# Two unused tiles that shift the right half of SBUF: 224 bytes for every pool there, 128 more for one

## The chip, the cores and the metric

The kernel runs on one core of a Trainium2 chip. The metric is the device time of one execution in microseconds (us). SBUF, the on-chip memory, has 128 partitions; an address below is the byte offset inside a partition, the same for all 128.

## The reference

One layer of a decoder trunk over 2,048 tokens of width 1,024, in float32, batch 1:

```python
mod = silu(c) @ w_ada + b_ada                      # shift, scale, gate, twice
u = rmsnorm(h, norm1_w) * (1 + sc1) + sh1
hq, hf, hi, hg, aq, ak, av = split(u @ w_in)       # 1024 -> 3584
o_hg = hgrn2(hq, hf, hi, hg)                       # 4 heads, state 128x128, chunks
o_da = diff_attention(aq, ak, av)                  # 4 heads, 2 softmaxes each, causal, ALiBi
h = h + g1 * (concat(o_hg, o_da) @ w_out)
u = rmsnorm(h, norm2_w) * (1 + sc2) + sh2
h = h + g2 * ((silu(u @ w_gate) * (u @ w_up)) @ w_down)   # inner width 2816
return rmsnorm(h, final_norm_w)
```

## The kernel before

**Products in three parts.** Nearly all matrix products are made with the type float32r. Every operand is split (`split`, L114 and L115) into a high part, a cast by ACT, and a low part, the rest, which DVE subtracts. A product is then three matmuls: high by high, high by low, low by high. Of a matmul, one operand is stationary (128 x 128, loaded into the array by a weight load that runs beside the matmul before it) and one is moving (128 x 256 or 128 x 512, streamed through).

**The lines with the matmuls.**

- L162, in `proj_ft`: 24 matmuls of 512 columns per accumulation; stationary are the weights wh and wl, moving the activations uh and ul. It serves attention's queries and keys and the recurrence's q and f. L408 is the same at the start of the kernel.
- L174, in `proj_tf`: 24 matmuls of 256 columns per accumulation, two accumulations a call; stationary are the activations, moving the weights. It serves the values, the recurrence's i and g, and the output projection.
- L603 and L604, attention's scores: stationary is q, moving ks, up to 512 columns.
- L629 and L633: attention's transposes and its product with the values, in plain float32, 128 columns.
- L985, in `seven`: the gate and up projections. A 2 x 2 block product is made with seven products in place of eight, each of 12 matmuls with 512 columns; stationary are the weights or their sums (wh2 and wl2; sh and sl for the seventh product), moving combinations of the activations (cx, cy, cu, ct2, ct3, ct4). In the first product the last matmul is cut into two halves of 256 columns. `seven` is called 44 times: two halves of the tokens, 11 pairs of weight blocks, gate and up.
- L1079, in `down`: the down projection, four blocks of 512 tokens, 22 inner blocks each, 24 matmuls of 512 columns for one; stationary are the activations sh and sl, moving the weights wh2 and wl2.

**The stages.** From 0 to some 400 us the norms and attention's projections; to some 1,130 us attention, with the recurrence and its projections put between its steps; then the output projection; and from some 1,400 us on the feed-forward part for the second half of the tokens (`seven`, then `down`), and again for the first half. TensorE's instructions run in the order of the program. The tile framework sets all waits, by the tiles that instructions read and write and by the memory that a tile takes over from an older one.

**Where tiles lie.** Pools are stacked from two sides. On the left, from address 16,512 on: the constants, puA, and then, one stage after the other, puB and px, pk and pp, pu7 and pt5. On the right, from 229,344 downwards: pw and pwD, ph, pf, px2, ps. Inside a pool the tiles lie in the order of their first use, from low addresses to high, each rounded up to 32 bytes. Nearly all large tiles have a multiple of 512 bytes, so one number says where the operands of a pool start:

| Pool | Side | What of it goes into matmuls | Start modulo 512 |
| --- | --- | --- | --- |
| puA, puB, pu7 | left | activations: uh, ul, all of cx, cy, cu, ct2, ct3, ct4 | 256 |
| pk | left | ks, q, the values vt | 256 |
| const | left | ident | 128 |
| pp | left | s, wt | 256, 96 |
| pw, pwD, pf | right | weights: wh, wl, wh2, wl2 | 480 |
| ph | right | the recurrence's Q, K, KM, KT | 352 |
| ps | right | sh, sl | 96 |

Between the lowest right pool and the highest left one there are at least 2,496 free bytes in every stage.

Of the kernel before, what the change touches and what calls it, by code (L numbers as in the profile page):

```python
# [9 lines left out]
F32 = mybir.dt.float32  # L10
# [9 lines left out]
P = 128  # L20
# [28 lines left out]
def kernel(ctx: ExitStack, tc: tile.TileContext, io: dict, out: bass.AP):  # L49
# [12 lines left out]
    dram = ctx.enter_context(tc.tile_pool(name="dram", bufs=1, space=DRAM))  # L62
    psum = ctx.enter_context(tc.tile_pool(name="psum", bufs=1, space=PSUM))
    puA = ctx.enter_context(tc.tile_pool(name="puA", bufs=1))
    early, later = ExitStack(), ExitStack()
    pw = early.enter_context(tc.tile_pool(name="pw", bufs=2, side="right"))

    def bank(tag, bufs, shape=(512,)):
        return psum.tile([P, *shape], F32, name=f"ps_{tag}", tag=tag, bufs=bufs)
# [16 lines left out]
    def bcast_row(ap):  # L86
        return ap.partition_broadcast(P)
# [745 lines left out]
    ps = ctx.enter_context(tc.tile_pool(name="ps", bufs=1, side="right"))  # L833

    def slots(names):

        n = [0]

        def take(dt=F32):
            two = []  # L840
            for c in range(2):
                tag = names[n[0] % len(names)]
                n[0] += 1
                two.append((puA if tag[0] == "u" else pu7).tile([P, TB], dt, name="slot", tag=tag, bufs=1))
            return two
        return take
# [104 lines left out]
    def temp():  # L951
        return pt5.tile([P, TB], F32, name="t512", tag="t512", bufs=NTMP)
# [89 lines left out]
    def down_step(b, f, at):  # L1042

        t = at()
        SP.dma_start(out=t, in_=act_d[b][f])
        return f, split_small(t), split_big(load_big(w_down[f * P:(f + 1) * P, None, :], 1))

    def down(b, at, first, others=(), after=()):

        others = iter(others)
        tags = (("acc", 2), ("acc", 2), ("sc", 2), ("sc", 2), ("hg", 2), ("hg", 2), ("pv", 1), ("tr", 1))
        pds = [bank(*t) for t in tags]
        place = slots([f"u{z}{k}" for z in "hl" for k in range(4)])
        ho = [place() for tt in range(NT)]
        place = slots(T4[4:])
        fw, g2 = place(), place()
        ws = []
        for f in range(NF):  # L1060
            ws.append(first.pop(0) if first else down_step(b, f, at))
            next(others, None)
            if f == 8:
                for c in range(2):
                    cs = slice(c * TB, (c + 1) * TB)
                    SP.dma_start(out=g2[c], in_=gate_d[1][:, cs])
                    SP.dma_start(out=fw[c], in_=bcast_row(io["final_norm_w"][cs]))
                    for tt in range(NT):
                        SP.dma_start(out=ho[tt][c], in_=h_d[b][tt * P:(tt + 1) * P, cs])

            if NF - (LAST if b else LAST0) <= f < NF - 1:
                continue
            for tt in range(NT):
                tsl = slice(tt * P, (tt + 1) * P)
                for cc in ((0,), (1,)) if not b and f == NF - 1 else ((0, 1),):
                    for g, a, w in ws:
                        for m, (x, y) in enumerate(((0, 0), (0, 1), (1, 0))):
                            for c in cc:
                                PE.matmul(  # L1079
                                    pds[2 * tt + c], a[x][:, tsl], w[y][:, c * TB:(c + 1) * TB],  # L1080
                                    start=g == 0 and m == 0, stop=g == NF - 1 and m == 2,
                                )
            ws = []
        for _ in others:
            pass
        made = after() if after else None

        def norm(tt):
            ss = ps.tile([P, 2], F32, name="fss", tag="fss", bufs=4)
            for c in range(2):  # L1090
                junk = ps.tile([P, TB], BF16, name="junk", tag="junk", bufs=1)
                ACT.activation(junk, ho[tt][c], AF.Square, accum_out=ss[:, c:c + 1])
            r = ps.tile([P, 1], F32, name="f_r", tag="f_r", bufs=2)
            DVE.tensor_tensor(r, ss[:, 0:1], ss[:, 1:2], op=ALU.add)
            DVE.tensor_scalar(r, r, 1.0 / D, EPS, op0=ALU.mult, op1=ALU.add)
            POOL.tensor_tensor(r, r, mhalf[:, :1], op=ALU.pow)
            for c in range(2):
                DVE.scalar_tensor_tensor(ho[tt][c], ho[tt][c], r, fw[c], op0=ALU.mult, op1=ALU.mult)
                (POOL if b else SP).dma_start(
                    out=out[0, b * TB + tt * P:b * TB + (tt + 1) * P, c * TB:(c + 1) * TB], in_=ho[tt][c]  # L1100
                )

        for tt in range(NT):
            ts = [temp() for c in range(2)]
            for c in range(2):
                DVE.tensor_tensor(ts[c], pds[2 * tt + c], g2[c], op=ALU.mult)
                if not b:
                    DVE.tensor_tensor(ho[tt][c], ho[tt][c], ts[c], op=ALU.add)
            if b:
                for c in range(2):  # L1110
                    DVE.tensor_tensor(ho[tt][c], ho[tt][c], ts[c], op=ALU.add)
            if not b:
                norm(tt)
        return made, (lambda: [norm(tt) for tt in range(NT)]) if b else None

    def calls(*fs):

        for f in fs:
            f()
            yield  # L1120
# [21 lines left out]
    two = [down_step(1, f, at1) for f in range(2)]  # L1142
    two, norms = down(1, at1, two, after=lambda: [down_step(0, f, at0) for f in range(2)])
    down(0, at0, two, calls(norms))


_INS = [
# [38 lines left out]
```

## Time and profile before

| What | Value |
| --- | --- |
| Time of 3 runs | 2808.2, 2809.4 and 2815.19 us, median 2809.4 |
| The profiled execution | 2806.66 us, of it the span 2804.8 us |
| Mean granted TensorE clock | 0.988 of full |
| TensorE busy | 2706.7 us, 97% of the span |
| Weight loads busy | 2320.0 us, 83% |
| DVE, ACT, POOL busy | 1709.4, 1124.3, 327.4 us |
| DMA | 403.52 MB, mean 144 GB/s |

PE is TensorE's matmuls, PEld its weight loads, DVE VectorE, ACT ScalarE, POOL GpSimd, SP SyncE, which issues most DMAs. The matmuls are pipelined: one starts before the one ahead has ended, so the duration of one is longer than its distance to the next. "L985" is line 985 of the kernel. `ps_acc<-cxh,wh` is a matmul that writes the PSUM tile ps_acc from moving cxh and stationary wh. The chain of waits is followed back from the last instruction, at each step to what released it.

### The profile page before, as it was taken

The page shows a single profiled execution, that of the slowest core. Times are in us where ns is not written, and L with a number is a line of the kernel's source. Part 1 is how long each engine was busy: PE and PEld are TensorE (multiplying, and loading weights), DVE is VectorE, ACT ScalarE, POOL GpSimd, SP SyncE. Part 2 cuts the span into 40 slices and gives each one's busy share as a digit, 9 for nine tenths or more (in the row PEclk, how much of TensorE's full clock was granted, in tenths as well). Part 3 has the DMA queues.
Part 4 walks back from the last instruction along what each step waited for, and adds up shares of the span by engine and source line. Part 5 has one row for each costly group of instructions (what it writes and reads, how often), then busy time and mean ns, then how long its engine had stood idle before and what let it go on. Part 6 is the DMA issues. An engine that isn't in the chain of part 4 may idle for free.

```text
span 2804.8 us, 40363 instructions
## 1 busy us (share of the span) xinstructions
PE 2706.7 (97%) x15017; PEld 2320.0 (83%) x15017; DVE 1709.4 (61%) x3456; ACT 1124.3 (40%) x2062; POOL 327.4 (12%) x493
## 2 busy tenths in 40 slices
PE   6999999999999998898999999999999999999998
PEld 5888879999999997897878888878887888888886
DVE  6434557777777779664585555553757555554354
ACT  4542135565565666543342222242433222222232
POOL 2552200000010000112210000020101000000010
PEclk9999999999999999998999999999999999999999
DMA  8765672434234220656542222274845222226461
GB/s 274 262 210 171 215 224 79 136 121 132 80 117 143 72 91 31 220 178 224 171 129 89 76 75 83 83 281 150 299 132 162 86 75 79 79 83 221 140 217 61
DMA packets 306104, 403.52 MB, mean 144 GB/s; under 512 B 22970, under 2 KB 208620, under 8 KB 305780
## 3 DMA queue, kind: packets, MB, share of 16 engines
q1 hardware_dynamic: 276788, 307.60, 34.4%
q0 software_dynamic: 29120, 93.35, 9.0%
q8 instruction: 118, 1.93, 0.3%
q14 instruction: 78, 0.64, 0.1%
HBM read 309.63 MB, written 91.23 MB: 143 GB/s over the span
## 4 chain that ended last, share of the span: by engine, by line
PE 74%; DMA 4%; DVE 4%; issue 3%; ACT 1%; POOL 1%; SPq 0%; POOLq 0%; DVEq 0%; ACTq 0%
PE ps_sc L985 8%; PE ps_hg L985 8%; PE ps_acc L985 8%; PE ps_acc L174 8%; PE ps_acc L162 5%; PE ps_acc L1079 4%; PE ps_sc L1079 4%; PE ps_hg L1079 4%; PE ps_pv L633 4%; PE ps_pv L1079 2%; PE ps_tr L985 2%; PE ps_pv L985 2%; PE ps_tr L1079 2%; PE ps_tr L629 2%; PE ps_sc L603 2%
## 5 line engine op out<-in xcount | busy, mean ns | idle before, releaser
L115 DVE TENSOR_TENSOR wl<-wraw,wh 128x1024 fp32r<-128x1024 f32 x252 | 307.5, 1221 | 98.4 <-ACT wh L114 94.9
L114 ACT CAST wh<-wraw 128x1024 fp32r<-128x1024 f32 x252 | 263.6, 1047 | 221.3 <-PE ps_acc L174 111.5
L174 PE MATMUL ps_acc<-wh,uh 128*128 128x256 f32 x1040 | 295.5, 286 | 0.8 <-ACT uh L505 0.6
L174 PE MATMUL ps_acc<-wl,uh 128*128 128x256 f32 x1040 | 293.8, 284 | 2.1 <-DVE wl L115 2.1
L174 PE MATMUL ps_acc<-wh,ul 128*128 128x256 f32 x1040 | 292.3, 284 | 0.0
L114 ACT CAST wh<-wsum 128x1024 fp32r<-128x1024 f32 x88 | 92.3, 1049 | 307.5 <-issue 142.7
L174 PEld LDWEIGHTS ps_acc<-wl,uh 128*128 128x128 f32 x1040 | 196.0, 189 | 4.9 <-DVE wl L115 2.3
L174 PEld LDWEIGHTS ps_acc<-wh,uh 128*128 128x128 f32 x1040 | 195.7, 189 | 3.8 <-ACT uh L505 1.4
L174 PEld LDWEIGHTS ps_acc<-wh,ul 128*128 128x128 f32 x1040 | 194.9, 189 | 2.3 <-issue 0.2
L115 DVE TENSOR_TENSOR sl<-slot,sh 128x512 fp32r<-128x512 f32 x88 | 60.5, 690 | 203.3 <-ACT sh L114 200.0
L612 ACT ACTIVATE s<-s,mx 128x2048 f32<-128x2048 f32 (+15 forms) x128 | 154.0, 1203 | 47.0 <-DVE mx L607 45.3
L607 DVE CUSTOM_DVE_ANT_0 s<-ps_sc,dist,mx 128x512 f32<-128x512 f32 x192 | 143.5, 748 | 44.1 <-PE ps_sc L604 39.6
L114 ACT CAST sh<-slot 128x512 fp32r<-128x512 f32 x88 | 54.2, 620 | 259.2 <-PE ps_tr L1079 217.5
L633 PE MATMUL ps_pv<-vt,wt 128*128 128x128 f32 x1088 | 150.8, 278 | 3.3 <-ACT wt L631 3.1
L633 PEld LDWEIGHTS ps_pv<-vt,wt 128*128 128x128 f32 x1088 | 140.4, 194 | 11.0 <-ACT wt L631 5.9
L115 DVE TENSOR_TENSOR wl<-wsum,wh 128x1024 fp32r<-128x1024 f32 x88 | 107.5, 1222 | 68.7 <-ACT wh L114 65.7
L162 PE MATMUL ps_acc<-ul,wh 128*128 128x512 f32 x352 | 141.9, 404 | 1.0 <-DMA ul<-ud 1.0
L162 PE MATMUL ps_acc<-uh,wh 128*128 128x512 f32 x352 | 142.1, 406 | 0.0
L1027 POOL DMA_DIRECT2D actd<-t x88 | 47.9, 544 | 798.1 <-DVE t L1026 793.8
L162 PE MATMUL ps_acc<-uh,wl 128*128 128x512 f32 x352 | 140.3, 400 | 0.4 <-DVE wl L115 0.4
L985 PE MATMUL ps_hg<-cuh,wh 128*128 128x512 f32 x352 | 139.6, 397 | 0.0
L985 PE MATMUL ps_hg<-cul,wh 128*128 128x512 f32 x352 | 139.5, 396 | 0.0
(406 smaller groups left out, 7028.1 us busy)
## 6 DMA issues: line engine op xcount, KB each, us to landing
wraw<-in_w_in_dram SPq DMA_DIRECT2D x88, 512.0 KB, 4.2
wraw<-in_w_ffn_down_dram SPq DMA_DIRECT2D x88, 512.0 KB, 3.7
wraw<-in_w_ffn_gate_dram SPq DMA_DIRECT2D x44, 512.0 KB, 3.9
wraw<-in_w_ffn_up_dram SPq DMA_DIRECT2D x44, 512.0 KB
actd<-t POOLq DMA_DIRECT2D x88, 256.0 KB, 2.5
slot<-actd SPq DMA_DIRECT2D x88, 256.0 KB, 5.0
ada_w<-in_w_ada_dram SPq DMA_DIRECT2D x64, 256.0 KB, 3.9
wraw<-in_w_out_dram SPq DMA_DIRECT2D x32, 512.0 KB, 4.2
```

Source lines behind the costliest of these rows:

```text
L114: ACT.copy(dst_h, src)
L115: DVE.tensor_tensor(dst_l, src, dst_h.bitcast(F32), op=ALU.subtract)
L162: PE.matmul(pa, a[:, k % 4, j * P:(j + 1) * P], c, start=n == 0, stop=n == 3 * NK - 1)
L174: PE.matmul(pa[:, j], a[:, tt * P:(tt + 1) * P], c[:, k % 4], start=n == 0, stop=n == 3 * NK - 1)
L603: PE.matmul(ps[:, :n], qs[m][0][:, qc], ks[m][pc][:, :n], start=True, stop=False)
L607: DVE.tensor_tensor_reduce(out=s[:, lo:hi], in0=ps[:, :hi - lo], in1=dist[:, u0_:u0_ + hi - lo], op0=ALU.add, op1=ALU.min, scale=-slope, s ...
L612: ACT.activation(s[:, :W], s[:, :W], AF.Exp, scale=-1.0, bias=mx[:, npiece - 1:npiece], accum_out=mx[:, 4:5])
L629: PE.transpose(out=pt[:, j - g], in_=S[0][:, j * P:(j + 1) * P], identity=ident)
L633: PE.matmul(pv[:, :P], wt[:, j - g], vq[j // 4][:, j % 4], start=j == 0, stop=j == i)
L985: PE.matmul(pa[:, cs], a, c[:, cs], start=first and i == 0, stop=i == 11 and cs.stop == TB, skip_group_check=not first)
L1027: POOL.dma_start(out=act_d[2 * s + t][2 * p + j], in_=a)
L1079: PE.matmul(pds[2 * tt + c], a[x][:, tsl], w[y][:, c * TB:(c + 1) * TB], start=g == 0 and m == 0, stop=g == NF - 1 and m == 2,)
```

## The change

Two tiles are reserved that no instruction reads or writes. The first is in a pool of its own, the outermost on the right side, 56 float32 a partition, kept for the whole kernel. The second is the last tile of the pool ps, 32 float32 a partition.

```diff
     puA = ctx.enter_context(tc.tile_pool(name="puA", bufs=1))
+
+    align = ctx.enter_context(tc.tile_pool(name="align", bufs=1, side="right"))
+    align.tile([P, 56], F32, name="align")
     early, later = ExitStack(), ExitStack()
     pw = early.enter_context(tc.tile_pool(name="pw", bufs=2, side="right"))
...
     two, norms = down(1, at1, two, after=lambda: [down_step(0, f, at0) for f in range(2)])
     down(0, at0, two, calls(norms))
+    ps.tile([P, 32], F32, name="align")
```

## Rows read from the trace of the kernel before

**Rows 1.** The page, part 1: busy time, share of the span and instructions of each engine.
```profile
PE 2706.7 (97%) x15017; PEld 2320.0 (83%) x15017; DVE 1709.4 (61%) x3456; ACT 1124.3 (40%) x2062; POOL 327.4 (12%) x493
```

**Rows 2.** The page, part 4: the chain that ended last, by engine and by line.
```profile
PE 74%; DMA 4%; DVE 4%; issue 3%; ACT 1%; POOL 1%; SPq 0%; POOLq 0%; DVEq 0%; ACTq 0%
PE ps_sc L985 8%; PE ps_hg L985 8%; PE ps_acc L985 8%; PE ps_acc L174 8%; PE ps_acc L162 5%; PE ps_acc L1079 4%; PE ps_sc L1079 4%; PE ps_hg L1079 4%; PE ps_pv L633 4%; PE ps_pv L1079 2%; PE ps_tr L985 2%; PE ps_pv L985 2%; PE ps_tr L1079 2%; PE ps_tr L629 2%; PE ps_sc L603 2%
```

**Rows 3.** Stretches: start:end, us; busy us (instructions) of PE, PEld, DVE, ACT, POOL; PEclk.
```profile
400.00:1100.00 700.00, 692.87 (x4864) 638.84 (x4863) 539.91 (x1548) 415.32 (x895) 51.16 (x53) 1.00 0.32 104
...
1400.00:1860.00 460.00, 452.81 (x1973) 363.80 (x1972) 281.53 (x405) 147.47 (x219) 41.21 (x70) 0.99 0.33 107
```

**Rows 4.** A stretch of 15 calls of seven(), L985 alone: PE busy (matmuls), PEclk.
```profile
1526.52:1820.62 294.10, 294.10 (x1276) 1.00 0.26 82
```

**Rows 5.** A stretch of down(), L1079 alone: PE busy (matmuls), PEclk.
```profile
1877.59:2088.00 210.41, 210.41 (x906) 1.00 0.60 203
```

**Rows 6.** The chain of waits in the output projection: start us, us, what.
```profile
1171.55 34.08 PE ps_acc L174 x288
```

**Rows 7.** The chain of waits in the mixed stage, 708 to 734 us.
```profile
708.68 0.23 PE ps_sc L603
...
709.37 0.23 PE ps_sc L604
...
714.72 4.43 PE ps_acc L162 x19
...
723.22 0.23 PE ps_sc L603
...
723.91 0.23 PE ps_sc L604
```

**Rows 8.** The chain of waits in seven(): the seventh product behind another one.
```profile
2243.43 2.33 PE ps_hg L985 x10
2245.76 2.81 PE ps_sc L985 x12
...
2251.13 2.80 PE ps_hg L985 x12
```

**Rows 9.** Timeline of PE, two runs of attention's scores: start us, us, instruction.
```profile
481.37 0.40 PE L604 MATMUL ps_sc<-ks,q 128*128 128x512 f32 x1
...
482.08 0.38 PE L730 MATMUL ps_hg<-hv,A__4567 128*128 128x128 f32 x2
...
669.62 0.39 PE L604 MATMUL ps_sc<-ks,q 128*128 128x512 f32 x1
...
670.32 0.28 PE L174 MATMUL ps_acc<-wh,uh 128*128 128x256 f32 x1
```

**Rows 10.** Line 115: duration ns min/median/max, first and last start.
```profile
L115 DVE TENSOR_TENSOR sl<-slot,sh x88: 677/693/695, 1852.5 to 2768.8; 128x512 fp32r<-128x512 f32 x88
...
L115 DVE TENSOR_TENSOR cul<-t,cuh x16: 682/684/693, 1393.2 to 2130.1; 128x512 fp32r<-128x512 f32 x16
```

**Rows 11.** DMA issues: count, KB each, median us to landing.
```profile
wraw<-in_w_in_dram SPq DMA_DIRECT2D x88, 512.0 KB, 4.2
...
xt<-in_x_dram SPq DMA_DIRECT2D x32, 256.0 KB, 4.5
```

**Rows 12.** The chain of waits, its longest pieces: two waits for weights.
```profile
1135.87 6.70 DMA wraw<-in_w_out_dram
...
2132.58 5.89 DMA wraw<-in_w_ffn_up_dram
```

**Rows 13.** Timeline of PE behind a wait.
```profile
1423.01 0.63 PE L985 MATMUL ps_hg<-cuh,wl 128*128 128x512 f32 x1
1423.43 0.63 PE L985 MATMUL ps_hg<-cuh,wh 128*128 128x512 f32 x1
1423.86 0.63 PE L985 MATMUL ps_hg<-cul,wh 128*128 128x512 f32 x1
```

**Rows 14.** That stretch, columns as in rows 3: PEclk is the granted clock.
```profile
1420.40:1423.80 3.40, 2.34 (x5) 1.78 (x6) 3.40 (x6) 3.06 (x6) 1.11 (x3) 0.58 0.57 169
```

## The prediction

> **What bounds the kernel now.** I read the page's busy table first [rows 1]: TensorE is busy for 97% of the span, the weight loads beside it for 83%, DVE for 61%. The chain of waits [rows 2] runs through TensorE for 74%, while DMA and DVE have 4% each and no line outside the matmuls reaches 2%. The stretches [rows 3] say that this holds in the mixed stage (attention beside the recurrence, 692.87 of 700 us busy) and in the gate and up projections (452.81 of 460 us). So the time is a row of matmuls, one behind the other, and the quantity to look at is the distance from one matmul to the next. The mean durations in the tables of groups (around 396 ns for 512 columns) don't show it, because the matmuls overlap; stretches in which TensorE runs one line without a gap do:
>
> - 512 columns at L985: 15 calls of seven() in 294.10 us [rows 4]. A call has 7 products of 12 matmuls (one of the 84 is split into two halves), so 294.10 / (15 x 84) = 233.4 ns.
> - 512 columns at L1079: 906 in 210.41 us [rows 5], 232.2 ns.
> - 256 columns at L174: 288 in 34.08 us [rows 6], 118.3 ns.
> - 512 columns at L162: 19 in 4.43 us [rows 7], 233.2 ns.
>
> How often: L162 has 1,392 of them (58 accumulations of 24), L408 another 144, L985 44 calls x 84 = 3,696, L1079 4 blocks x 22 x 24 = 2,112, L174 80 x 48 = 3,840. With these distances that is 1,536 x 233.3 + 3,696 x 233.4 + 2,112 x 232.2 + 3,840 x 118.3 ns = 358 + 863 + 490 + 454 = 2,165 us, 77% of the span. One nanosecond on each 512-column matmul is 7.3 us.
>
> **The change part by part.** No instruction, wait or DMA is added, removed or moved: the two tiles are never written. What moves is addresses. The first filler takes 56 x 4 = 224 bytes at the outer end of the right side, so each right pool lies 224 bytes lower: pw, pwD and pf go from 480 to 256 modulo 512, ph from 352 to 128, px2 from 288 to 64. The second adds 32 x 4 = 128 bytes at the upper end of ps (a pool's tiles lie in the order of their first use, and this one comes last), so ps goes from 96 by 224 + 128 to 256. The left pools stay at 256. The free gaps between the two sides hold kilobytes, and the shift of ps by 128 against px2 lets each large tile of ps still cover the same old tiles, so I count no new wait.
>
> What has another relative offset afterwards (moving start minus stationary start, modulo 512; slices inside a tile are multiples of 512 bytes) is then: L162, L408 and six of seven products of L985, now 288; the seventh product of L985 (stationary sh, sl), now 160; L1079, now 384; L174, now 224. All become 0. Attention's scores (L603, L604: ks and q, both in pk) are at 0 already, and so are Q, K, KM and KT among themselves. These are the rows that answer the question, since they are the same kind of instruction at the offset to which the change takes the others.
>
> The price of the offset, by rows. At 160 the twelve matmuls take 2.81 us, 234.2 ns each; at 288 ten in front of them take 2.33 us and twelve soon after 2.80 us, 233.0 and 233.3 ns [rows 8]. At 384 it is 232.2 ns [rows 5]. So the offset is worth about 2 ns from best to worst. At 0 there are only short runs. On the chain two runs of four stand, from 708.68 and from 723.22, each 0.92 us long [rows 7]: 230 ns, with 2.5 ns of rounding either way. By start times two other runs give 482.08 - 481.37 = 0.71 and 670.32 - 669.62 = 0.70 us for three matmuls [rows 9], 236.7 and 233.3 ns, with 3 ns of rounding. (The first of each run is left out there: its start lies early, while the operation in front of it still streams.) I take the mean of the four runs, 232.5 ns, which lies among the distances at the other offsets: 5,232 matmuls x (232.5 - 233.4) = -4.7 us for L162, L408 and L985, 2,112 x (232.5 - 232.2) = +0.6 us for L1079. For L174 I take 0: its 118.3 ns is half of the 512-column distance within 2 ns, so no separate cost of the weight load at its own offset stands out. Sum: -4 us.
>
> Bounds of the same terms: at 227.5 ns (the lower edge of the chain's rows) 5,232 x -5.9 + 2,112 x -4.7 = -41 us, and half of 5.9 for each of L174, 3,840 x -2.9 = -11 us, together -52 us. At 236.7 ns, 5,232 x 3.3 + 2,112 x 4.5 = +27 us, and 3,840 x 1.6 = +6 us, together +33 us. Nothing hides these: where TensorE has no gap, each of them counts in full.
>
> [...]
>
> The other engines: DVE's subtraction takes a median of 693 ns into ps at 96 and 684 ns into the left side at 256, over 512 columns [rows 10]; even if all of that 9 ns came from the address, DVE is idle for a third of the time beside the matmuls. DMAs into the right side: 512 KB of weights land in 4.2 us at an offset of 480, 256 KB of x in 4.5 us at 256 [rows 11], so a skewed target isn't dear here. I cost both at nothing; were every weight load quicker by a fifth, the five long pieces of the chain that wait for one, 4.5 to 6.7 us each (the first and the last of the five are shown) [rows 12] and 28 us together, would give 6 us.
>
> [...]
>
> **The total.** The profiled execution took 2806.66 us, 1.9 us of it around the span; the median of the runs is 2809.4 us, 2.7 us above. -4 us gives 2803 against the profile and 2805 us against the median, which I take. A measurement here tells about 0.3% (8.4 us) from no change.
>
> **The rivals.**
>
> 1. *The reads get out of each other's way (faster).* Each distance holds an excess: at the half clock matmuls follow each other in 0.42 to 0.43 us (1423.01, 1423.43, 1423.86) [rows 13], in a stretch with a mean granted clock of 0.58 [rows 14], so at the full clock 512 columns would be about 213 ns, and 20 ns are something else. If a part of it, 3 to 6 ns, is the weight load meeting the moving stream in the same rows of memory, offset 0 may end it in steady runs that attention's short ones don't show. For it: the steady distance does depend on the offset. Against: of the four runs at offset 0 only two lie lower, and both near 230 ns. At 229.5 ns: 5,232 x -3.9 + 2,112 x -2.7 = -26 us, 2783 us against the median. Chance 0.28.
> 2. *The whole excess goes (faster).* 20 x 5,232 + 19 x 2,112 + 11.7 x 3,840 ns = 190 us, 2620 us. [...] Against it: offset 0 exists in attention and keeps at least 227.5 ns; and the excess goes with the columns (20 ns on 512, 11.7 on 256) and not with the number of weight loads, which is one for each in both. Chance 0.03.
> 3. *Offset 0 is the bad one (slower).* Both reads now walk the same low addresses from their starts, so each weight load can meet the stream at its beginning, every time. Place: all of L985, L1079, L162 and L174; price: up to 236.7 ns, as the dearest run [rows 9], +27 to +33 us, 2836 to 2842 us, and some 2830 us at two thirds of it. It decides from 1.2 ns on each 512-column matmul on (8.4 / 7,344). Against: the chain's runs at the same offset, at 230 ns [rows 7]. Chance 0.13.
> 4. *The fillers don't shift what they should*, for instance because the last tile of ps lies at its lower end: then L1079 and the seventh product keep an offset, and the rest moves as above. Within 2 us of the forecast. Chance 0.02.
>
> No change worth measuring: 0.54, and 0.02 of rival 4. So faster 0.31, same 0.56, slower 0.13. The likeliest case alone spans 2799 to 2814 us. The range for 8 in 10 reaches from 2774 (rival 1 with most of its bound) to 2824 us (half of rival 3).
>
> **What would show it.** The same stretches after: 15 calls of seven() in 292 to 295 us and 906 matmuls of L1079 in 210 to 212 us would be my forecast; 289 us or less for the former is rival 1, 297 us or more rival 3. The runs of L603 and L604, L629 and L633 and the durations of DVE and ACT should not move at all. If L985 gains while L1079 loses, or L174 changes by over 2 ns each, the term was sized from the wrong rows. If the time moves while these distances stay, another part of the address shift (DMA, or a wait that I counted as absent) did it.

## The result and the profile after

Four runs of the changed kernel took 2768.53 to 2771.36 us, median 2769.77; four of the kernel before, beside them, 2808.2 to 2815.19, median 2811.67. The ratio is 0.9851, with a 95% interval of 0.9834 to 0.9868: 42 us faster. The prediction was 2805 us, with a range from 2774 on, and the time lies below it. The lines of the code stand 3 further down after the change: L162 is L165, L174 is L177, L603 and L604 are L606 and L607, L985 is L988, L1079 is L1082.

The profiled execution took 2769.06 us, 2767.2 of it the span. The busy table and the chain of the changed kernel, for [rows 1 and 2]:

```profile
PE 2668.8 (96%) x15017; PEld 2324.2 (84%) x15017; DVE 1709.2 (62%) x3456; ACT 1123.5 (41%) x2062; POOL 328.8 (12%) x493
...
PE 74%; DMA 4%; issue 3%; DVE 3%; ACT 1%; POOL 1%; SPq 1%; POOLq 0%; DVEq 0%; ACTq 0%
```

TensorE's busy time fell by 37.9 us (2706.7 to 2668.8) and the span by 37.6; the rest of the span, in which TensorE is idle, is 98.4 us where it was 98.1. DVE, ACT and POOL are busy for the same time within 1.4 us. So the whole gain lies inside the rows of matmuls. The stretches of [rows 4 and 5], with the same matmuls in them, L988 and then L1082 of the changed kernel:

```profile
1522.27:1808.37 286.10, 286.10 (x1277) 1.00 0.26 85
...
1864.13:2069.36 205.23, 205.23 (x906) 1.00 0.62 208
```

15 calls of `seven` take 286.10 us in place of 294.10, that is 286.10 / (15 x 84) = 227.1 ns for a matmul of 512 columns, 6.3 less. 906 matmuls of L1082 take 205.23 in place of 210.41 us, 226.5 ns, 5.7 less. The granted clock is 1.00 in both, before and after.

The 256-column matmuls went the other way. The chain of the changed kernel in the output projection, for [rows 6], and behind it three pieces of L165 in the mixed stage (start us, us, what):

```profile
1168.79 34.55 PE ps_acc L177 x288
...
597.99 0.92 PE ps_acc L165 x4
...
602.36 1.85 PE ps_acc L165 x8
...
609.58 2.50 PE ps_acc L165 x11
```

288 of L177 take 34.55 us where they took 34.08: 120.0 ns for one, 1.6 more. L165's pieces say something else: 230 ns at four matmuls, 231 at eight, 227.3 at eleven. The piece of eleven is cheaper for each matmul than the two short ones. The timeline of TensorE shows where the difference lies, at the start of a product of `seven` that follows a pair of 256-column matmuls (start us, us, instruction):

```profile
1473.04 0.40 PE L988 MATMUL ps_tr<-ct2h,wh 128*128 128x512 f32 x1
1473.28 0.40 PE L988 MATMUL ps_tr<-ct2l,wh 128*128 128x512 f32 x1
1473.51 0.39 PE L988 MATMUL ps_tr<-ct2h,wl 128*128 128x512 f32 x1
1473.74 0.40 PE L988 MATMUL ps_tr<-ct2h,wh 128*128 128x512 f32 x1
1473.97 0.39 PE L988 MATMUL ps_tr<-ct2l,wh 128*128 128x512 f32 x1
1474.20 0.39 PE L988 MATMUL ps_tr<-ct2h,wl 128*128 128x512 f32 x1
1474.43 0.39 PE L988 MATMUL ps_tr<-ct2h,wh 128*128 128x512 f32 x1
1474.66 0.39 PE L988 MATMUL ps_tr<-ct2l,wh 128*128 128x512 f32 x1
1474.88 0.39 PE L988 MATMUL ps_tr<-ct2h,wl 128*128 128x512 f32 x1
1475.11 0.39 PE L988 MATMUL ps_tr<-ct2h,wh 128*128 128x512 f32 x1
1475.34 0.39 PE L988 MATMUL ps_tr<-ct2l,wh 128*128 128x512 f32 x1
1475.56 0.39 PE L988 MATMUL ps_tr<-ct2h,wl 128*128 128x512 f32 x1
```

The first six distances are 0.23 to 0.24 us, 1.39 us together (232 ns each), nearly as at the old offset (233); the five from 1474.43 on are 1.13 us together, 226 ns. Such a run *settles*: only after some matmuls is the distance shorter by 6 ns. What the two reads do meanwhile, no row shows. Taken from the exact starts of all of L988's runs in the trace, the mean distances from the first of a run on are 233, 235, 229, 232, 231, then 227 and it stays there. In the kernel before, L985 at an offset of 288 starts with 236, 234, 232, 235, 234, 234 and goes on between 232 and 235: it never settles.

Means over the whole trace, from the start of one matmul to the start of the next of the same line and width, without the distances that hold a pause (over a quarter above the median), and the sum:

| Line, columns | Count | Before, ns | After, ns | us |
| --- | --- | --- | --- | --- |
| L162, L408 (now L165, L411), 512 | 1,536 | 233.1 | 228.0 | -7.9 |
| L985 (L988), 512 | 3,696 | 233.3 | 227.1 | -22.9 |
| L1079 (L1082), 512 | 2,112 | 232.4 | 226.7 | -11.8 |
| L174 (L177), 256 | 3,840 | 118.3 | 119.6 | +4.9 |

Together -37.7 us, against -37.6 in the span; one profile of each kernel doesn't tell tenths, so an agreement this close is chance.

### The profile page after: what moved, and what is told of

Same layout as the page of the kernel before. It is cut to its first block, busy times and chain, and to the rows that moved or that the text cites. A ratio compares the mean times of both kernels' runs of the same rounds, so it can differ in the third digit from the quotient of the medians.

```text
span 2767.2 us, 40363 instructions
## 1 busy us (share of the span) xinstructions
PE 2668.8 (96%) x15017; PEld 2324.2 (84%) x15017; DVE 1709.2 (62%) x3456; ACT 1123.5 (41%) x2062; POOL 328.8 (12%) x493
## 4 chain that ended last, share of the span: by engine, by line
PE 74%; DMA 4%; issue 3%; DVE 3%; ACT 1%; POOL 1%; SPq 1%; POOLq 0%; DVEq 0%; ACTq 0%
PE ps_acc L177 8%; PE ps_sc L988 8%; PE ps_hg L988 8%; PE ps_acc L988 8%; PE ps_acc L165 5%; PE ps_acc L1082 4%; PE ps_sc L1082 4%; PE ps_hg L1082 4%; PE ps_pv L636 4%; PE ps_pv L1082 2%; PE ps_tr L988 2%; PE ps_pv L988 2%; PE ps_tr L1082 2%; PE ps_tr L632 2%; PE ps_sc L606 2%
## 5 line engine op out<-in xcount | busy, mean ns | idle before, releaser
L177 PE MATMUL ps_acc<-wh,uh 128*128 128x256 f32 x1040 | 298.1, 288 | 2.1 <-DVE lo L328 1.3
L177 PE MATMUL ps_acc<-wl,uh 128*128 128x256 f32 x1040 | 297.0, 287 | 0.4 <-DVE wl L118 0.4
L177 PE MATMUL ps_acc<-wh,ul 128*128 128x256 f32 x1040 | 294.8, 287 | 0.0
L177 PEld LDWEIGHTS ps_acc<-wh,uh 128*128 128x128 f32 x1040 | 199.0, 192 | 5.5 <-DVE lo L328 1.8
L177 PEld LDWEIGHTS ps_acc<-wl,uh 128*128 128x128 f32 x1040 | 199.4, 192 | 3.3 <-DVE wl L118 0.6
L177 PEld LDWEIGHTS ps_acc<-wh,ul 128*128 128x128 f32 x1040 | 198.3, 192 | 2.6 <-issue 0.5
L165 PE MATMUL ps_acc<-ul,wh 128*128 128x512 f32 x352 | 139.9, 398 | 2.5 <-DMA ul<-ud 2.5
L165 PE MATMUL ps_acc<-uh,wh 128*128 128x512 f32 x352 | 140.4, 401 | 0.0
L165 PE MATMUL ps_acc<-uh,wl 128*128 128x512 f32 x352 | 138.5, 395 | 0.3 <-DVE wl L118 0.3
L988 PE MATMUL ps_hg<-cul,wh 128*128 128x512 f32 x352 | 137.9, 392 | 0.1
L988 PE MATMUL ps_hg<-cuh,wh 128*128 128x512 f32 x352 | 137.8, 392 | 0.0
```

What stands on the lines that cost most here:

```text
L165: PE.matmul(pa, a[:, k % 4, j * P:(j + 1) * P], c, start=n == 0, stop=n == 3 * NK - 1)
L177: PE.matmul(pa[:, j], a[:, tt * P:(tt + 1) * P], c[:, k % 4], start=n == 0, stop=n == 3 * NK - 1)
L988: PE.matmul(pa[:, cs], a, c[:, cs], start=first and i == 0, stop=i == 11 and cs.stop == TB, skip_group_check=not first)
```

## The experiments

Two theories came first. **A**: the distance depends on the relation of the two operands, moving start minus stationary start. **B**: it depends on where an operand starts in itself, and 256 is a good place for the right side. Later **E** came up for differences that are no matter of the matmuls: transfers into and out of tiles that start askew are dearer. All runs are of whole kernels; each ratio is against the kernel before on the same chip.

**Only the right side's filler.**

```diff
 two, norms = down(1, at1, two, after=lambda: [down_step(0, f, at0) for f in range(2)])
 down(0, at0, two, calls(norms))
-ps.tile([P, 32], F32, name="align")
```

> The filler of ps is left out; the one at the outer end of the right side stays. L1082 and the seventh product then have an offset of 384 (stationary at 384, moving at 256), all other split products 0. Theory A (the distance between two matmuls depends on moving start minus stationary start modulo 512, and at 0 a run settles at 226.8 ns): L1082 keeps the 232.4 ns that it had at the same offset before, so 2,112 x 5.6 = 11.8 us over the changed kernel; the seventh product (528) loses 2 to 3 us and each product behind it settles anew, about 1 us: 2785 us. Rival B (what counts is that a right tile starts on a multiple of 64 or 128 bytes, whatever the other operand): ps starts at 384, a multiple of both, so no loss: 2770 us.

2786.75 us, ratio 0.9913 (0.9897 to 0.9929). The same two stretches of this kernel, L988 and L1082:

```profile
1523.95:1811.75 287.80, 287.80 (x1276) 1.00 0.26 84
...
1868.78:2079.16 210.38, 210.38 (x906) 1.00 0.61 203
```

L1082 stays at 232.2 ns (210.38 / 906), as before the change, with its operands at an offset of 384. Six of seven products in L988 gain, the seventh (232.9 ns) doesn't, and the others settle anew behind it (227.7 in place of 227.1). That is A, and the second filler's share: 17 us between the two medians.

**Only ps's filler.** Both operands of down then start at 480, at offset 0; the seventh product of `seven` goes from an offset of 160 to 288, and everything else is as before.

```diff
-    align = ctx.enter_context(tc.tile_pool(name="align", bufs=1, side="right"))
-    align.tile([P, 56], F32, name="align")
```

> Only the filler of ps, so ps lies at 480 like the weights: L1080 has offset 0 with both operands at 480; all others keep the offsets of the kernel before (288, 224), the seventh product has 288 in place of 160. Theory A: L1080 settles at 226.8 ns although nothing there starts on a multiple of 64, 2,112 x 5.6 = 11.8 us below before: 2800 us. Rival B (absolute start): no gain, 2811 us.

2796.75 us, ratio 0.9948 (0.9933 to 0.9962). L986, L1080 and, from the chain of waits, 288 matmuls of L175 in this kernel:

```profile
1529.45:1823.45 294.00, 294.00 (x1276) 1.00 0.26 82
...
1880.99:2086.20 205.21, 205.21 (x906) 1.00 0.63 208
```
```profile
1173.76 34.08 PE ps_acc L175 x288
```

L1080 has 226.5 ns with both operands at 480, L986 its old 233.3, L175 its old 118.3 with its old offset of 224. B falls.

**Everything at 480.** The left side moves instead.

```diff
-    align = ctx.enter_context(tc.tile_pool(name="align", bufs=1, side="right"))
-    align.tile([P, 56], F32, name="align")
...
     a2 = const.tile([P, NK], F32, name="a2")
+    const.tile([P, 56], F32, name="skew")
```

> No filler on the right; 224 bytes more in the constants shift the left side from 256 to 480, and the filler of ps stays, so all operands of the split products start at 480 modulo 512 and the offset is 0 everywhere. Theory A: as the changed kernel, 2770 us, 226.8 ns at 512 columns and 119.6 ns at 256. Rival B: 2811 us or more, since now the left side is skewed as well. Rival C (DMA or DVE and ACT gain from targets on a multiple of 64): also 2811 us.

2781.09 us, ratio 0.9887 (0.9871 to 0.9904). The distances are those after the change (226.8, 228.0, 227.1 and 119.6 ns). The two stretches of this kernel, L987 and L1081:

```profile
1532.71:1818.81 286.10, 286.10 (x1277) 1.00 0.27 85
...
1874.57:2079.81 205.24, 205.24 (x906) 1.00 0.63 208
```

So the distance follows the offset, as A says. Its 2770 us is missed by 11 us, none of it in steady rows.

**Which offsets are as good as 0.** The slots of the weights become 128 bytes longer, so that one tag's slots start at offsets of 0, 128, 256 and 384; hx has 3 buffers in place of 4 to make room.

```diff
-        wh = pool.tile([P, 4, 256], F32R, name="wh", tag=th, bufs=bufs)
-        wl = pool.tile([P, 4, 256], F32R, name="wl", tag=tl, bufs=bufs)
+        wide = 1024 + 32
+        wh = pool.tile([P, wide], F32R, name="wh", tag=th, bufs=bufs)
...
+        wl = pool.tile([P, wide], F32R, name="wl", tag=tl, bufs=bufs)
...
+        w = D + 32 if tag in ("wh2", "wl2") else D
```

> The changed kernel with each slot of the weights wh, wl (three each) and wh2, wl2 (four each) longer by 128 bytes, and two buffers of x2 less one in the output projection for the room; so the weights of successive runs of 12 matmuls start at 256, 384, 0 and 128 modulo 512, and one execution has offsets 0, 128, 256 and 384 side by side. Theory A: only runs at 0 go to 227 ns within 12 matmuls, those at 128, 256 and 384 stay at 231 to 235 ns. Rival D (a multiple of 256, or of 128, is enough): 256, or all four, go to 227 ns. At 256 columns I expect 119 to 120 ns at 0 and 117 to 119 ns elsewhere. The time itself, about 2790 us, decides nothing.

One run, 2793.0 us. Pieces of the chain in down, six matmuls each, at offsets of 256, 384, 128 and 0 in this order:

```profile
1992.05 1.36 PE ps_hg L1096 x6
...
1996.16 1.40 PE ps_sc L1096 x6
...
2001.76 1.40 PE ps_sc L1096 x6
...
2008.69 1.36 PE ps_hg L1096 x6
```

256 is as good as 0 (1.36 us, 227 ns), 128 and 384 are not (1.40 us, 233 ns). By exact starts, late in a run: 226.8 to 227.2 ns at 0, 226.7 to 227.5 at 256, 232.9 to 233.2 at 128, 232.0 to 233.5 at 384. At these four offsets the distance repeats after 256 bytes and not after 512.

**All at 288, all at 320, and 256 apart.** Three kernels on one chip: the left side further by 32, 64 and 256 bytes; in the first two the right side's filler is so much shorter that it follows, in the third only the left moves, to 0, and the offset is 256 everywhere but in down's own operands. The edit is that at 288; at 320 the two tiles have 40 and 16 float32, and 256 apart 56 (as in the changed kernel) and 64.

```diff
-    align.tile([P, 56], F32, name="align")
+    align.tile([P, 48], F32, name="align")
...
+    const.tile([P, 8], F32, name="skew")
```

> As the run with both sides at 480, whose matmul distances were those of the changed kernel but which took 11 us more: here 32 bytes more in the constants put the left side at 288, a filler of 192 bytes the right side, and ps keeps its 128; the offset is 0 everywhere and every large tile starts 32 past a multiple of 64. Theory E (skew costs the DMAs, whose long waits at the stages' borders TensorE sees): 2778 to 2783 us, as at 480, with matmuls at 226.8 ns. Rival F (480 was dear for another reason, such as a chance order of transfers): 2770 us.

> The same with 64 bytes on the left, 160 on the right, 128 in ps: all at 320, a multiple of 64 but not of 128; offset 0 everywhere. Theory E with a border of 64 bytes: 2770 us. If only multiples of 128 or 256 are cheap: 2778 to 2783 us. Rival F: anything between, with no order among 256, 288, 320 and 480.

> The changed kernel with 256 bytes more in the constants, so that the left side starts at 0 and the right side stays at 256: offset 256 for L166, L178, L412 and L989; L1083, with both operands on the right, stays at 0. Theory A in the form that the scan by 128 left (the period is 256 bytes, not 512): 2770 us and 227 ns in steady runs of L989. Rival (the 227 ns at 256 in the scan came only from its neighbours at 0, in whose steady state the run began): 231 to 234 ns, 2795 to 2800 us.

2778.45 us, ratio 0.9881 (0.9863 to 0.99), at 288; 2781.12, 0.9898 (0.9874 to 0.9922), at 320; 2770.62, 0.9851 (0.9831 to 0.987), at 256 apart. TensorE is busy for 2672.2, 2671.6 and 2671.3 us in them, within 1 us of each other. The 15 calls, at L989, and the 906 of L1083 in the last one, 227.1 and 226.5 ns for a matmul as in the changed kernel:

```profile
1519.89:1805.99 286.10, 286.10 (x1277) 1.00 0.26 85
...
1863.59:2068.79 205.20, 205.20 (x906) 1.00 0.62 208
```

So 256 apart is as good as 0 in the whole kernel. For E, a border of 64 bytes, at which 320 should have been cheap, falls. For what separates the three, the busy tables of the kernels at 480, 288, 320 and 256 apart, in this order:

```profile
PE 2673.5 (96%) x15017; PEld 2325.4 (84%) x15017; DVE 1708.8 (61%) x3456; ACT 1123.2 (40%) x2062; POOL 329.4 (12%) x493
```
```profile
PE 2672.2 (96%) x15017; PEld 2326.4 (84%) x15017; DVE 1708.8 (62%) x3456; ACT 1126.2 (41%) x2062; POOL 328.6 (12%) x493
```
```profile
PE 2671.6 (96%) x15017; PEld 2325.3 (84%) x15017; DVE 1708.9 (61%) x3456; ACT 1123.6 (40%) x2062; POOL 327.8 (12%) x493
```
```profile
PE 2671.3 (96%) x15017; PEld 2324.0 (84%) x15017; DVE 1708.9 (62%) x3456; ACT 1124.0 (41%) x2062; POOL 328.6 (12%) x493
```

With spans of 2780.2, 2776.3, 2779.4 and 2768.3 us TensorE is idle for 106.7, 104.1, 107.8 and 97.0 us; it is 98.4 in the changed kernel. So 7 to 11 us of the 8 to 12 us that lie between the span 256 apart and the other three are idle time. Where it stands, the chains of waits show for two of the kernels, at 480 and at 256 apart: a piece of 12 matmuls of `proj_ft` starts at 405.54 and 399.69 us, one of 24 of `proj_tf` at 1003.32 and 996.60 us, and the 288 of the output projection at 1176.56 and 1165.09 us. So 5.9 us of the difference are there by 405 us, 6.7 by 1,003 and 11.5 by 1,177. That transfers are the cause is E's account and not shown.

**Finer offsets.** The slots become 32 bytes longer, in the manner of the 128.

```diff
+        wide = 1024 + 8
...
+        w = D + 8 if tag in ("wh2", "wl2") else D
```

> The scan with slots 32 bytes longer: offsets 0, 32, 64 and 96 at L1096 and L190, and 0, 480, 448 and 416 at L1002, side by side in one execution. If settling needs a multiple of 256 exactly, only the runs at 0 reach 227 ns, and those at 32, 64 and 96 stay at 231 to 235 ns; if small offsets are as good as none, 32 (and 480) go to 227 ns too, and the distance grows step by step towards 128. At 256 columns 117 to 120 ns in all of them. The time, near 2790 us, decides nothing.

One run, 2802.37 us. What the two scans say together, by exact starts (512 columns late in a run, 256 columns the mean over all):

| Offset | 512 columns, ns | 256 columns, ns |
| --- | --- | --- |
| 0 | 227 | 119.3 |
| 32 | 233.3 | 117.4 |
| 64 | 228.9 | 116.8 |
| 96 | 233.5 | 119.8 |
| 128 | 233 | 118.8 |
| 256 | 227 | 119.1 |
| 384 | 233 | 118.8 |
| 416, 448, 480 | 233.8, 233.2, 233.5 | not run |

For 512 columns 0 and 256 are best and 64 settles in part. For 256 columns those two are among the dearer ones, and 64 is best.

**The best of both.** Slots are 256 bytes longer, so that all keep their start modulo 256, and weights for `proj_tf` lie 64 bytes into their slot (a shift of 16 float32 at its loads, one of which is shown); this is for 3,456 of its 3,840 matmuls, hx at 3 buffers. Beside it a control with hx at 3 buffers alone, and a kernel with all operands at 384 (left side 128 bytes further).

```diff
-        wh = pool.tile([P, 4, 256], F32R, name="wh", tag=th, bufs=bufs)
-        wl = pool.tile([P, 4, 256], F32R, name="wl", tag=tl, bufs=bufs)
+        wide = 1024 if suffix else 1088
+        wh, wl = (
+            pool.tile([P, wide], F32R, name=n, tag=t, bufs=bufs)[:, (shift if wide > 1024 else 0):][:, :1024].rearrange(
+                "p (k c) -> p k c", c=256)
+            for n, t in (("wh", th), ("wl", tl))
+        )
...
-            w = load_wd(3072 + p * 256)
+            w = load_wd(3072 + p * 256, 16)
...
-            return px.tile([P, 2, 256], F32, name="hx", tag="ho", bufs=4)
+            return px.tile([P, 2, 256], F32, name="hx", tag="ho", bufs=3)
```

> Two fillers kept; the slots of wh/wl and wh2/wl2 are 256 bytes longer, and 3,456 of proj_tf's 3,840 matmuls of 256 columns read weights 64 bytes into their slot (offset 64 or 320, that is 64 modulo 256). To make room hx has 3 buffers instead of 4. Theory A (the distance depends on the offset modulo 256, and 256 columns are cheapest at 32 and 64): these matmuls go from 119.6 to 116.6 ns apart, 3,456 x 3.0 = 10.4 us, so 2759 us (from 2769.8), with the products of 512 columns unchanged at 227 to 228 ns. Rival B (256 columns stand at 116.6 only where the run before it was of the kernel with skewed slots, and the time there is set by the wait for weights): about 2769. Theory E (DMAs whose SBUF side starts off a multiple of 256 bytes are dearer): nothing, since the weights' raw tiles, which the DMAs write, stay at multiples of 256.

```diff
-            return px.tile([P, 2, 256], F32, name="hx", tag="ho", bufs=4)
+            return px.tile([P, 2, 256], F32, name="hx", tag="ho", bufs=3)
```

> The control of e9: the changed kernel with hx at 3 buffers instead of 4, nothing else. If the fourth buffer is not needed: 2770 us, within 2 us. If writing out waits for a buffer, some us more, which then have to be added to what e9 shows.

```diff
-    align.tile([P, 56], F32, name="align")
+    align.tile([P, 24], F32, name="align")
...
+    const.tile([P, 32], F32, name="skew")
```

> Left side 128 bytes further (both operands at 384, offset 0 everywhere). The distances between matmuls stay as after the change in every theory (226.7, 228.0, 227.1, 119.6). Theory E with a border of 256 bytes: DMA packets dearer by some 2 per cent and 2778 to 2781 us, as with 288, 320 and 480. Theory E with a border of 128 bytes: 2770 us, as with 256 and 0. No theory of the matmuls alone tells 384 from 256: 2770.

At 64: 2771.71 us, ratio 0.9867 (0.9847 to 0.9887). The control: 2778.18, 0.9892 (0.9874 to 0.991). At 384: 2774.28, 0.9882 (0.9867 to 0.9897). The same 288 matmuls in the chain of the first and of the control:

```profile
1163.65 33.93 PE ps_acc L181 x288
```
```profile
1173.94 34.55 PE ps_acc L177 x288
```

117.8 against 120.0 ns; over all at 64 the mean is 117.6, so 3,456 x 2.0 = 6.9 us, and the medians differ by 6.5. But the granted clock differs too: the four runs at 64 have 0.986 to 0.99, three of the control's four 0.985, and at 0.988 each kernel has one run, of 2774.51 us at 64 and 2774.03 without. So the 6.5 us are no measure of the 2 ns. The expected 116.6 ns, and with it 2759 us, are missed: here 64 gives a nanosecond less than in the scan (117.6 ns against 116.8), and no row shows why. The control itself is 8.4 us above the changed kernel's median; in the profiles the span is 9.5 us longer, of which idle time is some 2 us (100.7 against 98.4), and the rest is busy time, at the same 120.0 ns for these 288, with a mean granted clock of 0.985 in place of 0.987. In the kernel at 384 TensorE is busy for 2676.2 us, at a granted clock of 0.985, where the control at the same clock has 2676.0 (2776.7 - 100.7); with a span of 2775.0 that leaves an idle time of 98.8 us, like 256 and 0:

```profile
PE 2676.2 (96%) x15017; PEld 2328.8 (84%) x15017; DVE 1708.6 (62%) x3456; ACT 1124.1 (41%) x2062; POOL 330.0 (12%) x493
```

**The same with hx at 4 buffers, and the changed kernel again.** Only pw's slots are longer here, for 1,920 matmuls at 64; the changed kernel ran on the same chip.

```diff
-        wide = 1024 if suffix else 1088
+        wide = 1024 if pool is not pw or suffix else 1088
...
-            return px.tile([P, 2, 256], F32, name="hx", tag="ho", bufs=3)
+            return px.tile([P, 2, 256], F32, name="hx", tag="ho", bufs=4)
```

> The best of both without the cost of e10: the two fillers, hx at 4 buffers, and only the slots of wh/wl in pw 256 bytes longer, so that 1,920 of proj_tf's 3,840 matmuls of 256 columns read weights 64 bytes into their slot (64 modulo 256); project_out's 1,536 and the rest stay at 0. Theory A: these go from 119.6 to 117.6 ns apart as in e9, 1,920 x 2.0 = 3.9 us below the changed kernel on the same chip, 2766 us; all other distances as after the change. Rival B (the gain between e9 and e10 came from elsewhere): as the changed kernel.

> The changed kernel itself, so that e12 has it beside it on one chip: 2770 us by every theory of the matmuls. Were it some 5 to 10 us off, the differences of that size among kernels with the same distances (2770 to 2781 us) would be no matter of where the operands start.

2769.35 us, ratio 0.986 (0.984 to 0.9881), against 2775.22 us (2769.46 to 2780.91), 0.9879 (0.986 to 0.9898). The busy tables, the version first:

```profile
PE 2665.6 (96%) x15017; PEld 2319.0 (84%) x15017; DVE 1708.8 (62%) x3456; ACT 1123.2 (41%) x2062; POOL 328.6 (12%) x493
```
```profile
PE 2671.1 (96%) x15017; PEld 2325.2 (84%) x15017; DVE 1708.3 (62%) x3456; ACT 1123.3 (41%) x2062; POOL 329.5 (12%) x493
```

TensorE is busy for 5.5 us less where 1,920 x 2.2 = 4.2 us were to be had (117.4 against 119.6 ns). Here too the clock takes part: 0.988 against 0.987 in these two profiles, and at 0.989 the version has runs of 2767.91 and 2769.87 us, the changed kernel one of 2769.46. Both pairs point the same way, but the intervals overlap in each, and at an equal clock, as far as its three digits tell, the gain isn't seen: that 64 is better for 256 columns is shown in the distances, that a kernel with it beats the changed one is not shown in the times.

The repeat also says how far a difference of kernels on different chips is to be trusted: one and the same kernel has medians of 2769.77 and 2775.22 us, and its five runs here go from 2769.46 at a mean granted clock of 0.989 to 2780.91 at 0.985. So the 11 us of the kernel at 480 are no proof of E by themselves. Nor do the times on one chip settle it: there 2778.45 and 2781.12 us stand against 2770.62 with the left side at 0, and a repeat of the changed kernel beside other runs gave 2775.22. What speaks for E is the idle time of one profile each: 104.1 to 107.8 us with the left side 32, 64 and 224 bytes past a multiple of 256, and 97.0 to 101.4 at 0, at 128 and in every kernel that leaves the left side at 256, but for the scan by 32 bytes (103.6), whose slots lie askew. Whether it is transfers, and which, and whether 128 bytes is the border, stays open.

## Why the prediction was wrong

- **What bounds the kernel, and how many matmuls**: right. The gain is the number of matmuls times the change of their distance (37.7 us, against 37.9 in TensorE's busy time), and TensorE's idle time did not move (98.1 and 98.4 us).
- **What moves**: right. The fillers shifted what they should (rival 4 is out), and the two experiments with one filler split the gain by the offsets that the prediction listed.
- **The price of offset 0**: here it failed, at "I take the mean of the four runs, 232.5 ns". The four runs of attention at offset 0 [rows 7 and 9] have four matmuls each, and a run at offset 0 needs some six to settle: 232 ns for its first six distances in the timeline above, 226 after. The rows were the right instruction at the right offset in the wrong place, and they have not changed, as the prediction said. Attention's own in the changed kernel, two of 512 columns behind two of 384 (start us, us, instruction):

```profile
709.60 0.40 PE L606 MATMUL ps_sc<-ks,q 128*128 128x512 f32 x1
709.84 0.39 PE L607 MATMUL ps_sc<-ks,q 128*128 128x512 f32 x1
710.07 0.60 PE L698 MATMUL ps_hg<-Q,KM 128*128 128x128 f32 x4
```

  0.24 and 0.23 us still. By exact starts the second and third distances in its runs of four are 232 and 233 ns before and 232 and 232 ns after. The forecast of -4 us for L162, L408, L985 and L1079 is -42.6 us measured (7.9 + 22.9 + 11.8). The text named the gap itself ("At 0 there are only short runs", and in rival 1 "steady runs that attention's short ones don't show") and gave it 0.28; what it lacked was a reason to let four short runs decide for 7,344 matmuls in long ones.
- **L174 at 0**: the second term that was mis-sized, "no separate cost of the weight load at its own offset stands out". The move from 224 to 0 costs 1.3 ns (118.3 to 119.6), 3,840 x 1.3 = +4.9 us; that it is the weight load is not shown. The halving of the 512-column distance was no argument: at 256 columns the order of the offsets is another one.
- **Rival 1** foresaw the gain, in steady runs that attention's short ones don't show, and it was larger than by its 229.5 ns: 226.7 to 228.0. Its reason, that the weight load meets the moving stream, is not shown: the runs show that the difference of the two starts decides, and not why. Its bound of 227.5 for the distance was nearly the truth, and -41 us for that term was a good figure; the range took in "most of its bound" and ended at 2774. **Rival 2** fell: 226.7 ns is still far from its 213, an estimate from the distances of 0.42 to 0.43 us [rows 13] at a granted clock that is 0.50 from 1423.00 to 1423.86 us. **Rival 3** fell for 512 columns (226.7 to 228.0 ns in place of 232.4 to 233.3) and holds, with 1.3 ns, for 256; its reason, two reads that walk the same addresses and meet at the stream's beginning, is in no row.
- **DVE and DMA at nothing**: right for this change. DVE's subtraction into ps, now at 256, and into the left side, unmoved, take 692 and 683 ns, within 1 ns of before [rows 10], so their difference was not the address; the landings [rows 11] stay where they were:

```profile
L118 DVE TENSOR_TENSOR sl<-slot,sh x88: 673/692/694, 1839.4 to 2731.7; 128x512 fp32r<-128x512 f32 x88
...
L118 DVE TENSOR_TENSOR cul<-t,cuh x16: 677/683/693, 1391.7 to 2110.1; 128x512 fp32r<-128x512 f32 x16
```
```profile
wraw<-in_w_in_dram SPq DMA_DIRECT2D x88, 512.0 KB, 4.0
...
xt<-in_x_dram SPq DMA_DIRECT2D x32, 256.0 KB, 4.7
```

## What to carry to other kernels

Where TensorE runs without a gap, look at where the two operands of a matmul start relative to each other in a partition: a few hundred unused bytes in one pool were worth 1.5% here, with the same instructions and waits. A price taken from another place in the trace needs the same run length as well as the same instruction and the same operands: look at the distances one by one, from the first of a run on, before a short run speaks for a long one. And size each width by its own rows, for what helped 512 columns by 5.1 to 6.2 ns cost 256 columns 1.3 ns here.

## What the runs showed of the hardware that was not expected

- In the runs of this case the distance between float32r matmuls of 512 columns went with moving start minus stationary start modulo 256 bytes: 227 to 228 ns at 0, 229 at 64, 232 to 234 at the others that were run. Where both start at an offset of 0 made no such difference: 15 calls of `seven` take 286.10 us with both at 256 and with both at 480, and TensorE is busy for 2668.8 us at 256, 2673.5 at 480, 2672.2 at 288, 2671.6 at 320 and 2676.2 at 384, at granted clocks of 0.985 to 0.988.
- At offset 0 it took five to nine matmuls until a run was at 227 ns (L988's from its sixth distance on, 226.9; L165's from its tenth on, 227.2). With the twelve of the seventh product at 384 in between, the other products of `seven` had 227.7 in place of 227.1 ns.
- With 256 columns the best of the offsets run is 64 (116.8 to 117.8 ns), and 0 is among the dear ones (119.3 to 120.0).
- Why the offset counts is not seen in any row; the offsets and distances are all that the runs show.
